# First mixer of a hybrid RG-LRU model: rounding moved to VectorE, splits ahead of square roots, decay series in the prologue, output-projection splits on GpSimd

## The chip, the cores and the metric

The kernel runs on one core of a Trainium2 chip. The metric is the device time of one execution in microseconds (us), as the median of several runs. TensorE (PE) does the matmuls, VectorE (DVE), ScalarE (ACT) and GpSimd (POOL) work on vectors, and SyncE (SP) issues most of the transfers. Each engine takes its own instructions strictly in order; semaphores let one wait for another.

## The reference, cut to what matters

The model has two layers. Layer 0 mixes tokens with a bidirectional gated recurrence (RG-LRU), layer 1 with a chunked gating MLP; each is followed by a mixture-of-experts layer (64 experts, 8 per token). There are 256 latent tokens and 256 context tokens, width 1024. The change lies in the mixer of layer 0:

```python
def lru_coeffs(u, r_w, r_b, i_w, i_b, lam, reset_first):
    r = sigmoid(einsum('bthi,hij->bthj', ub, r_w) + r_b)      # per head, 256x256
    ig = sigmoid(einsum('bthi,hij->bthj', ub, i_w) + i_b)
    log_a = LRU_C * r * log_sigmoid(lam)
    a = exp(log_a)
    mult = sqrt(-expm1(2.0 * log_a))
    return a, mult * ig * u

def rglru_mixer(hx, hc, w_in, conv_w, conv_b, r_w, r_b, i_w, i_b, lam, w_out, ctx_out):
    gate_x, ux = split(hx @ w_in, 2)
    ux = dwconv_centred(ux, conv_w, conv_b)                   # 4 taps
    uc = dwconv_centred(hc @ w_in[:, RNN_WIDTH:], conv_w, conv_b)
    yx = 0
    for d in range(2):                                        # both directions
        h_c = linear_scan(*lru_coeffs(flip(uc), ...))
        a_x, b_x = lru_coeffs(flip(ux), ...)
        b_x[:, 0] += a_x[:, 0] * h_c[:, -1]
        yx = yx + flip(linear_scan(a_x, b_x))
    return (gelu(gate_x) * yx) @ w_out
```

The recurrent width is 1280, in 5 heads of 256 channels. The result is scaled by a modulation vector, which is a matmul of the conditioning vector with large weights (`ada_w`), and added to the stream.

## The kernel before, in words

**Precision.** TensorE takes 32-bit numbers rounded to a shorter form (`F32R`). To keep full precision each operand is split in a high part (rounded) and a low part (the rest), and each product is three matmuls (`mm3`, L309): high by high, high by low, low by high. Weights come from memory as tiles of 128x2048 and are split in four pieces of 128x512 by `splitter` (L553): ScalarE casts the high part `wh` (L563), and VectorE or GpSimd subtracts to give the low part `wl` (L564). Which of the two subtracts is what `split_eng` says (L706): GpSimd for A and C of head 0 and for every second piece of O and Q, VectorE for all else. There are 7 buffers for each part. `wq(q)` emits splits up to piece q + 2, so `ready(n)` emits all pieces below n. Since every engine keeps its order, the place where a split is emitted sets its place in the queues of ScalarE and of the subtracting engine.

**Stages.** A prologue computes the normalisation and, in four quarters of 256 channels, the modulation (`first_quarter`, L718): ada matmuls, VectorE's normalise (L694), ScalarE's high part of the normalised input (L733), VectorE's low part (L744), and A's matmuls of head 0 on the quarters that are there. Then `plan0` lists the steps: for each head h

- A(h): input projection of the recurrent branch, two banks of 128x512 (latent and context tokens beside each other), then the convolution: ScalarE's first tap (L758), VectorE's three others (L760), the rounding `us` (L763, ScalarE) and its low part (L764, VectorE). At its end `roots` (L847) takes the square roots of the results that the head before has left (ScalarE, with a load of another function table).
- C(h): the gate projection, GELU on ScalarE, and `release` (L887): B_end of the head before, the scans on VectorE.
- B(h): the two gates of the recurrence (`T`, `I`), on the weights of the tile "gate", with tanh and exp on ScalarE, then four passes of 128x1024 on VectorE (L841 to L844). `gated` (L894) multiplies with GELU's result and splits into `zh` and `zl`, on GpSimd for heads 0 to 3, on VectorE for head 4.

Between these stand fillers F, the ada matmuls of later modulations (`s<-wr,stat` and `b<-wr,stat`), one tile of weights each. In the order of TensorE: A0 F C0 B0 F, A1 FFF C1 FF B1 F, A2 FF C2 FF B2 F, A3 FF C3 FF B3 F, A4 F C4 FF B4 FFFF. Then O0 to O3 do the output projection for the first four heads, Q adds head 4, and `Tail` (L575) adds to the stream, squares, and starts the router's matmuls.

**Decay.** `decay` (L790) computes log-sigmoid of `lam`, 128x20 numbers, as a series of small GpSimd steps, with one reciprocal (L795) and the last two steps on VectorE (L805, L806). It is called after A0 and before C0's and B0's work.

**Order of transfers.** Weight tiles go through 8 slots in the order of the plan, issued by SyncE; a tile's transfer starts when the tile eight before it has been freed.

Of the kernel before, what the change touches and what calls it, by code (L numbers as in the profile page):

```python
# [301 lines left out]
def _body(nc, tc, a, pp, rp, ps, ps1, dr):  # L302
# [334 lines left out]
    def mixer0(rx):  # L637
      with tc.tile_pool(name="m0", bufs=1) as mp, tc.tile_pool(name="m0t", bufs=2) as tp:
# [26 lines left out]
        for t_, n_ in ((cw, "a_cw"), (cb, "a_cb"), (rb_, "a_rb"), (ib_, "a_ib"), (lam, "a_lam")):  # L665
            nc.sync.dma_start(t_, a[n_])

# [38 lines left out]
        def split_eng(i, c):  # L706
            kind, j = plan0[users[i]]
            return G if kind in "AC" and j == 0 or kind in "OQ" and c % 2 else V

# [4 lines left out]
        def ready(n):  # L714

            wq(n - 3)

        def first_quarter(b):  # L718
# [30 lines left out]
        def A(h, q):  # L749
# [4 lines left out]
            def conv(i, p):  # L754
# [7 lines left out]
                of = o.rearrange("p s t -> p (s t)")  # L762
                S.copy(out=us[:, 0, i, :], in_=of)  # L763
                V.tensor_tensor(out=us[:, 1, i, :], in0=of, in1=us[:, 0, i, :].bitcast(F32), op=OP.subtract)  # L764
# [3 lines left out]
            for i, k in steps:  # L768
                if h == 0 and i == 0 and k:
                    yield  # L770
                wc = divmod(2 * k + i if h == 0 else 8 * i + k, 4)
                mm3(ps_[i], *cut(wq(q + wc[0], 4 if h == 0 and k < 7 else None), wc[1]), h0(0, k), h0(1, k), k == 0, k == 7)
                if k == 7:
                    ready(q + 8)
                    conv(i, ps_[i])
            roots()

# [4 lines left out]
        for b in range(1, 4):  # L782
            for _ in range(NEXT[b - 1]):
                next(a0)
            normalise(range(2 * b, 2 * b + 2))
            first_quarter(b)
        for t_ in (rb_, ib_):
            V.tensor_scalar(out=t_, in0=t_, scalar1=0.5, scalar2=None, op0=OP.mult)

        def decay():  # L790

            S.activation(out=s0, in_=lam, func=AF.Abs)
            S.activation(out=s0, in_=s0, func=AF.Exp, scale=-1.0)
            G.tensor_scalar(out=s1, in0=s0, scalar1=2.0, scalar2=None, op0=OP.add)
            V.reciprocal(out=s1, in_=s1)  # L795
            G.tensor_tensor(out=s0, in0=s0, in1=s1, op=OP.mult)
            G.tensor_tensor(out=s1, in0=s0, in1=s0, op=OP.mult)
            nterm = 9
            G.memset(s2, 1.0 / (2 * nterm + 1))
            for i in range(nterm - 1, -1, -1):  # L800
                G.tensor_tensor(out=s2, in0=s2, in1=s1, op=OP.mult)
                G.tensor_scalar(out=s2, in0=s2, scalar1=1.0 / (2 * i + 1), scalar2=None, op0=OP.add)
            G.tensor_tensor(out=s2, in0=s2, in1=s0, op=OP.mult)
            G.tensor_scalar(out=s1, in0=lam, scalar1=0.0, scalar2=-2.0, op0=OP.min, op1=OP.mult)
            V.scalar_tensor_tensor(out=nz, in0=s2, scalar=4.0, in1=s1, op0=OP.mult, op1=OP.add)  # L805
            V.tensor_scalar(out=nz2, in0=nz, scalar1=-2.0, scalar2=None, op0=OP.mult)  # L806

        def B(h, q):
# [92 lines left out]
        def O(i, q):  # L901
            ob[i] = bank()
            for j in range(2):
                for f in range(8):
                    mm3(ob[i][:, j * T:(j + 1) * T], *cut(wq(q + 2 * j + f // 4), f % 4), zh[:, f, :], zl[:, f, :],
                        j == 0 and f == 0, False)
            if i < 2:
                ready(q + 7)
                release()

# [12 lines left out]
        for i, (kind, j) in enumerate(plan0):  # L923
            if kind == "F":
# [3 lines left out]
                continue  # L928
            if kind == "O" and j == 0:
                tail = Tail(tp, 0, mod[:, 0, 2, :], rw, "hf", 4)  # L930
# [5 lines left out]
            if i == 0:  # L936
                deque(a0, 0)
                decay()
                continue
# [710 lines left out]
```

## Time and profile before

| what | us |
|---|---|
| median of 3 runs | 1522.29 (1521.48 to 1526.03) |
| profiled execution, its own time | 1523.33 |
| its span on the core | 1521.5 |
| PE busy | 1409.8 (93%) |
| DVE busy | 750.9 (49%) |
| ACT busy | 522.9 (34%) |
| POOL busy | 330.2 (22%) |
| prologue, to the end of A0 | 0 to 43.5 |
| heads 0 to 4, to the end of B4 | 43.5 to 224.5 |
| last fillers, O and Q | 224.5 to 277.3 |
| all that follows | 277.3 to 1521.5 |

The span is the time from the first to the last instruction in the trace; the execution's own time also has what lies around it. Busy shares are means over the span; the first mixer, some 277 us, has gaps of PE of its own, which the page's mean hides. In a timeline row the bracket at the end gives the idle time of the engine just before and the engine, tile and line that ended it.

### The profile page before, as it was taken

The page shows a single profiled execution, that of the slowest core. Times are in us where ns is not written, and L with a number is a line of the kernel's source. Part 1 is how long each engine was busy: PE and PEld are TensorE (multiplying, and loading weights), DVE is VectorE, ACT ScalarE, POOL GpSimd, SP SyncE. Part 2 cuts the span into 40 slices and gives each one's busy share as a digit, 9 for nine tenths or more (in the row PEclk, how much of TensorE's full clock was granted, in tenths as well). Part 3 has the DMA queues.
Part 4 walks back from the last instruction along what each step waited for, and adds up shares of the span by engine and source line. Part 5 has one row for each costly group of instructions (what it writes and reads, how often), then busy time and mean ns, then how long its engine had stood idle before and what let it go on. Part 6 is the DMA issues. An engine that isn't in the chain of part 4 may idle for free.

```text
span 1521.5 us, 27414 instructions
## 1 busy us (share of the span) xinstructions
PE 1409.8 (93%) x10752; PEld 983.7 (65%) x10752; DVE 750.9 (49%) x1412; ACT 522.9 (34%) x911; POOL 330.2 (22%) x420
## 2 busy tenths in 40 slices
PE   6798987789999999999999999978999999999998
PEld 4576757646557666565656899855656657566665
DVE  6488888622434433243345697542425334343434
ACT  4676764412322222222224535332213212222232
POOL 1200013421312222112201181232132212121210
PEclk9899998899999999999999999999999999999999
DMA  9575566559998999999999954449999999999994
GB/s 377 240 269 221 222 255 280 232 227 369 353 412 363 421 420 382 421 394 421 421 418 398 346 194 140 165 172 386 372 369 389 386 420 421 403 405 421 420 421 187
DMA packets 77444, 514.86 MB, mean 338 GB/s; under 512 B 9856, under 2 KB 10240, under 8 KB 17024
## 3 DMA queue, kind: packets, MB, share of 16 engines
q1 hardware_dynamic: 74720, 508.91, 82.8%
q10 hardware_dynamic: 2592, 4.16, 0.9%
q8 instruction: 86, 1.41, 0.4%
q14 instruction: 46, 0.38, 0.1%
HBM read 511.99 MB, written 1.05 MB: 337 GB/s over the span
## 4 chain that ended last, share of the span: by engine, by line
PE 56%; issue 13%; DMA 4%; POOL 3%; DVE 2%; ACT 1%; ACTq 0%; POOLq 0%; SPq 0%; DVEq 0%
PE b L307 46%; PE s L307 9%; DMA wr<-in_m_gu 3%; POOL S L1427 2%; POOL wl L564 1%; DMA wr<-in_m_dn 1%; PE b L1503 1%; DMA wx<-in_m_dn 1%; DVE wl L564 1%; DVE h L976 0%; ACT wh L563 0%; DVE v L1032 0%; DVE xT L1143 0%; DVE v L1095 0%; DVE u L984 0%
## 5 line engine op out<-in xcount | busy, mean ns | idle before, releaser
L307 PE MATMUL b<-wr,xg 128*32 128x512 f32 (+2 forms) x1512 | 306.8, 599 | 9.2 <-DMA wr<-in_m_gu 8.0
L564 POOL TENSOR_TENSOR wl<-wr,wh 128x512 fp32r<-128x512 f32 x81 | 111.5, 1388 | 560.2 <-ACT wh L563 533.3
L563 ACT CAST wh<-wr 128x512 fp32r<-128x512 f32 x260 | 152.1, 618 | 164.1 <-PE s L307 79.8
L564 DVE TENSOR_TENSOR wl<-wr,wh 128x512 fp32r<-128x512 f32 x179 | 141.1, 815 | 125.9 <-ACT wh L563 125.8
L307 PE MATMUL b<-wx,xg 128*32 128x512 f32 (+2 forms) x696 | 199.2, 598 | 0.9 <-ACT xg L1443 0.7
L307 PEld LDWEIGHTS b<-wr,xg 128*32 128x32 f32 (+2 forms) x1512 | 84.5, 118 | 141.3 <-issue 114.2
L307 PE MATMUL s<-hh,wh 128*128 128x256 f32 x512 | 153.1, 299 | 6.4 <-ACT wh L563 6.4
L307 PE MATMUL b<-wr,ht 128*32 128x512 f32 (+2 forms) x728 | 153.8, 596 | 2.7 <-ACT ht L1505 1.4
L1143 DVE SCALAR_TENSOR_TENSOR xT<-b,mod,xT 128x256 f32<-128x256 f32 x304 | 130.0, 479 | 48.9 <-PE b L307 43.0
L1519 DVE SCALAR_TENSOR_TENSOR Y<-b,gt,Y 128x512 fp32r<-128x512 f32 x88 | 66.1, 751 | 169.3 <-ACT Y L1518 169.3
L307 PE MATMUL s<-hh,wl 128*128 128x256 f32 x512 | 146.3, 286 | 3.4 <-POOL wl L564 3.4
L307 PE MATMUL s<-hl,wh 128*128 128x256 f32 x512 | 145.3, 284 | 0.0
L564 POOL TENSOR_TENSOR wl<-wx,wh 128x512 fp32r<-128x512 f32 x43 | 58.5, 1367 | 299.3 <-ACT wh L563 258.7
L307 PEld LDWEIGHTS s<-hh,wh 128*128 128x128 f32 x512 | 98.8, 193 | 36.0 <-issue 28.3
L1496 DVE TENSOR_TENSOR h<-h,b 128x256 f32<-128x256 f32 x44 | 18.5, 421 | 208.2 <-ACT h L1495 208.2
L1518 ACT ACTIVATE Y<-b,gt 128x512 fp32r<-128x512 f32 x88 | 60.5, 687 | 136.6 <-PE b L307 132.2
L1495 ACT ACTIVATE h<-b 128x256 f32<-128x256 f32 x44 | 16.9, 383 | 259.8 <-PE b L307 259.8
L307 PE MATMUL b<-wx,ht 128*32 128x512 f32 (+2 forms) x376 | 101.9, 596 | 0.8 <-ACT ht L1505 0.5
L307 PEld LDWEIGHTS s<-hh,wl 128*128 128x128 f32 x512 | 98.7, 193 | 4.5 <-POOL wl L564 4.2
L563 ACT CAST wh<-wx 128x512 fp32r<-128x512 f32 x108 | 64.6, 619 | 101.9 <-PE s L307 51.7
L307 PEld LDWEIGHTS s<-hl,wh 128*128 128x128 f32 x512 | 99.0, 193 | 0.4
L307 PE MATMUL b<-S,xt 128*128 128x256 f32 x704 | 94.1, 287 | 0.0
(283 smaller groups left out, 2773.9 us busy)
## 6 DMA issues: line engine op xcount, KB each, us to landing
wr<-in_m_gu SPq DMA_DIRECT2D x170, 1024.0 KB, 11.9
wx<-in_m_gu SPq DMA_DIRECT2D x86, 1024.0 KB, 12.1
wr<-in_m_dn SPq DMA_DIRECT2D x82, 1024.0 KB, 10.6
wx<-in_m_dn SPq DMA_DIRECT2D x40, 1024.0 KB, 11.3
wr<-in_ada_w SPq DMA_DIRECT2D x32, 1024.0 KB, 7.8
wr<-in_a_in SPq DMA_DIRECT2D x10, 1024.0 KB, 8.3
wr<-in_ada SPq DMA_DIRECT2D x8, 1024.0 KB, 12.2
wr<-in_b_v SPq DMA_DIRECT2D x6, 1024.0 KB, 14.8
```

What stands on the lines that cost most here:

```text
L307: PE.matmul(out, lhsT, rhs, start=start, stop=stop, skip_group_check=True)
L563: S.copy(out=hi, in_=t)
L564: eng(i, c).tensor_tensor(out=lo, in0=t, in1=hi.bitcast(F32), op=OP.subtract)
L1143: V.scalar_tensor_tensor(out=xT[:, d, :], in0=y, scalar=mod[:, l, 5, d:d + 1], in1=xT[:, d, :], op0=OP.mult, op1=OP.add)
L1427: (G if b else V).tensor_scalar(out=s[:, tt, i * P + o:i * P + o + wd], in0=C["iota1"][:, j:j + wd], scalar1=agq[:, tt, q:q + 1], scalar2= ...
L1495: S.activation(out=h, in_=p[:, :256], func=AF.Silu)
L1496: V.tensor_tensor(out=h, in0=h, in1=p[:, 256:], op=OP.mult)
L1503: PE.transpose(p[:, k * P:(k + 1) * P], h[:, k * P:(k + 1) * P], ident)
L1518: S.activation(out=hi, in_=p, func=AF.Copy, scale=gts[g])
L1519: V.scalar_tensor_tensor(out=y[:, 1, 512 * c:512 * c + 512], in0=p, scalar=gts[g], in1=hi.bitcast(F32), op0=OP.mult, op1=OP.subtract)
```

## The change

It touches the first mixer alone:

- The rounding `us` goes from ScalarE to VectorE.
- A emits three of the four splits of the gate tile ahead of `roots` (`ready(q + 11)`), where all four stood behind it.
- `decay` moves into the prologue, behind the second quarter, after three splits for A0 (`wq(1, 4)`). Its last two steps and the halving of the biases `rb_` and `ib_` move from VectorE to GpSimd; the reciprocal stays on VectorE.
- The five small loads (`cw`, `cb`, `rb_`, `ib_`, `lam`) are issued by ScalarE in place of SyncE.
- `split_eng` gives every low part of O to GpSimd and every low part of Q to VectorE.
- O emits its splits ahead of its matmuls, for all four groups, and the releases too.
- `Tail` is made at O2 in place of O0, so the scaling of the router's weights (`rws`) and its first matmuls come later.

```diff
@@ -663,7 +663,7 @@
         nc.sync.dma_start(mixg, a["mix_g"])
         st.grow(rp, "wr", RING)
         for t_, n_ in ((cw, "a_cw"), (cb, "a_cb"), (rb_, "a_rb"), (ib_, "a_ib"), (lam, "a_lam")):
-            nc.sync.dma_start(t_, a[n_])
+            S.dma_start(t_, a[n_])
 
         for half, e in ((0, pe[:, :16].rearrange("p (k r) -> p k r", k=4).unsqueeze(3).to_broadcast([P, 4, 4, 64])),
                         (1, pe[:, 16:].rearrange("p (k c) -> p k c", k=4).unsqueeze(2).to_broadcast([P, 4, 4, 64]))):
@@ -705,7 +705,7 @@
 
         def split_eng(i, c):
             kind, j = plan0[users[i]]
-            return G if kind in "AC" and j == 0 or kind in "OQ" and c % 2 else V
+            return G if kind in "AC" and j == 0 or kind == "O" else V
 
 
         base = 8
@@ -714,6 +714,25 @@
         def ready(n):
 
             wq(n - 3)
+
+        def decay():
+
+            S.activation(out=s0, in_=lam, func=AF.Abs)
+            S.activation(out=s0, in_=s0, func=AF.Exp, scale=-1.0)
+            G.tensor_scalar(out=s1, in0=s0, scalar1=2.0, scalar2=None, op0=OP.add)
+            V.reciprocal(out=s1, in_=s1)
+            G.tensor_tensor(out=s0, in0=s0, in1=s1, op=OP.mult)
+            G.tensor_tensor(out=s1, in0=s0, in1=s0, op=OP.mult)
+            nterm = 9
+            G.memset(s2, 1.0 / (2 * nterm + 1))
+            for i in range(nterm - 1, -1, -1):
+                G.tensor_tensor(out=s2, in0=s2, in1=s1, op=OP.mult)
+                G.tensor_scalar(out=s2, in0=s2, scalar1=1.0 / (2 * i + 1), scalar2=None, op0=OP.add)
+            G.tensor_tensor(out=s2, in0=s2, in1=s0, op=OP.mult)
+            G.tensor_scalar(out=s1, in0=lam, scalar1=0.0, scalar2=-2.0, op0=OP.min, op1=OP.mult)
+            G.tensor_scalar(out=s2, in0=s2, scalar1=4.0, scalar2=None, op0=OP.mult)
+            G.tensor_tensor(out=nz, in0=s2, in1=s1, op=OP.add)
+            G.tensor_scalar(out=nz2, in0=nz, scalar1=-2.0, scalar2=None, op0=OP.mult)
 
         def first_quarter(b):
 
@@ -760,7 +779,7 @@
                     V.scalar_tensor_tensor(out=o[:, :, d0:d1], in0=pv[:, :, s0_:s1_], scalar=cw[:, kk, ft:ft + 1],
                                            in1=o[:, :, d0:d1], op0=OP.mult, op1=OP.add)
                 of = o.rearrange("p s t -> p (s t)")
-                S.copy(out=us[:, 0, i, :], in_=of)
+                V.tensor_copy(out=us[:, 0, i, :], in_=of)
                 V.tensor_tensor(out=us[:, 1, i, :], in0=of, in1=us[:, 0, i, :].bitcast(F32), op=OP.subtract)
 
             ps_ = [bank(), bank()]
@@ -773,6 +792,7 @@
                 if k == 7:
                     ready(q + 8)
                     conv(i, ps_[i])
+            ready(q + 11)
             roots()
 
         held, rooted, done = deque(), deque(), []
@@ -784,27 +804,11 @@
                 next(a0)
             normalise(range(2 * b, 2 * b + 2))
             first_quarter(b)
+            if b == 1:
+                wq(1, 4)
+                decay()
         for t_ in (rb_, ib_):
-            V.tensor_scalar(out=t_, in0=t_, scalar1=0.5, scalar2=None, op0=OP.mult)
-
-        def decay():
...
-            V.scalar_tensor_tensor(out=nz, in0=s2, scalar=4.0, in1=s1, op0=OP.mult, op1=OP.add)
-            V.tensor_scalar(out=nz2, in0=nz, scalar1=-2.0, scalar2=None, op0=OP.mult)
-
+            G.tensor_scalar(out=t_, in0=t_, scalar1=0.5, scalar2=None, op0=OP.mult)
         def B(h, q):
             warm(AF.Exp)
             uc, us = ucs.pop(h)
@@ -900,13 +904,13 @@
 
         def O(i, q):
             ob[i] = bank()
+            ready(q + 7)
+            if i < 2:
+                release()
             for j in range(2):
                 for f in range(8):
                     mm3(ob[i][:, j * T:(j + 1) * T], *cut(wq(q + 2 * j + f // 4), f % 4), zh[:, f, :], zl[:, f, :],
                         j == 0 and f == 0, False)
-            if i < 2:
-                ready(q + 7)
-                release()
 
         def Q(_, q):
             wq(q + 1)
@@ -926,7 +930,7 @@
                 ada_step(l, c, k, tp)
                 wq(4 * sum(u < i for u in users) + 1)
                 continue
-            if kind == "O" and j == 0:
+            if kind == "O" and j == 2:
                 tail = Tail(tp, 0, mod[:, 0, 2, :], rw, "hf", 4)
             if kind == "O" and j == 2:
                 warm(AF.Sqrt)
@@ -935,7 +939,6 @@
                     gated(done.pop())
             if i == 0:
                 deque(a0, 0)
-                decay()
                 continue
             n = st.reserve({"A": "a_in", "C": "a_in", "B": "gate", "O": "a_out", "Q": "a_out"}[kind])
             deque({"A": A, "B": B, "C": Cg, "O": O, "Q": Q}[kind](j, 4 * users.index(n - base)) or (), 0)
```

How the rows of the engines move, at three places. ScalarE in head 1, from the convolution to C1's GELU (`uc` convolution, `us` its rounding, `wr_736` and `wr_737` the gate tile of head 1, `Tt` the held results of head 0), before:

```order
L758 ACTIVATE uc<-b,cb,cw 128x512
L763 CAST us<-uc 128x512
L758 ACTIVATE uc<-b,cb,cw 128x512
L763 CAST us<-uc 128x512
L851 ACT_TABLE_LOAD
L851 ACTIVATE Tt<-Tt 128x1024 x2
L563 CAST wh<-wr_736 128x512 x4
L880 ACT_TABLE_LOAD
```

and after:

```order
L777 ACTIVATE uc<-b,cb,cw 128x512 x2
L563 CAST wh<-wr_737 128x512 x3
L855 ACT_TABLE_LOAD
L855 ACTIVATE Tt<-Tt 128x1024 x2
L563 CAST wh<-wr_737 128x512
L884 ACT_TABLE_LOAD
```

Three of the four casts now stand ahead of the table load and the roots, and the two casts of `us` are gone from this queue.

VectorE in the prologue, from the second to the third quarter (`hf` and `wx` the low part of the input, `s_184` the decay's intermediate, `Tt` and `I` normalise), after:

```order
L759 TENSOR_SCALAR hf<-Tt,sx,mod 128x256
L759 TENSOR_SCALAR hf<-I,sc,modc 128x256
L763 TENSOR_TENSOR wx_103<-hf,wx_101 128x512
L723 RECIPROCAL s_184<-s_184 128x20
L694 TENSOR_TENSOR Tt<-xT,b 128x256 x2
```

and GpSimd at the same place, after:

```order
L564 TENSOR_TENSOR wl<-wr_128,wh 128x512 x4
L722 TENSOR_SCALAR s_184<-s_183 128x20
L724 TENSOR_TENSOR s_183<-s_183,s_184 128x20
L725 TENSOR_TENSOR s_184<-s_183 128x20
L727 MEMSET s_185 128x20
```

The reciprocal, which came after A0's convolution before, now stands between two quarters, and it needs GpSimd's first step (`s_184` at L722), which stands behind all four subtracts of A0's tile `wr_128`.

GpSimd from the end of the heads to Q (`zh` and `zl` of heads 2 and 3, `wr_1794` and `wr_1807` the first tile of O), before:

```order
L899 TENSOR_TENSOR zl<-hf,zh 128x512
L564 TENSOR_TENSOR wl<-wr_1794,wh 128x512
L898 CAST zh<-hf 128x512
L899 TENSOR_TENSOR zl<-hf,zh 128x512
L564 TENSOR_TENSOR wl<-wr_1794,wh 128x512
L564 TENSOR_TENSOR wl<-wr_1861,wh 128x512 x2
L564 TENSOR_TENSOR wl<-wx_1889,wh 128x512 x2
L564 TENSOR_TENSOR wl<-wx_1891,wh 128x512 x2
L564 TENSOR_TENSOR wl<-wx_1893,wh 128x512 x2
L618 TENSOR_TENSOR hf<-hf 128x256 x5
```

and after:

```order
L903 TENSOR_TENSOR zl<-hf,zh 128x512
L564 TENSOR_TENSOR wl<-wr_1807,wh 128x512 x2
L902 CAST zh<-hf 128x512
L903 TENSOR_TENSOR zl<-hf,zh 128x512
L564 TENSOR_TENSOR wl<-wr_1807,wh 128x512 x2
L564 TENSOR_TENSOR wl<-wr_1862,wh 128x512 x4
L564 TENSOR_TENSOR wl<-wx_1890,wh 128x512 x4
L564 TENSOR_TENSOR wl<-wx_1892,wh 128x512 x4
L618 TENSOR_TENSOR hf<-hf 128x256 x5
```

Every subtract of O is on this queue now, two of them ahead of head 3's `zh` where one was, and those of Q (the last row of `wx_1893` before) have left it.

## Rows read from the trace of the kernel before

**Rows 1.** Stretches: start to end, length, busy of each engine (count), PEclk, DMA share, GB/s.

```profile
43.50:73.80 30.30, 20.42 (x109) 16.29 (x112) 11.83 (x19) 17.52 (x29) 9.13 (x27) 0.83 0.56 226
...
310.70:1521.50 1210.80, 1155.90 (x9065) 785.88 (x9065) 514.52 (x988) 341.91 (x624) 263.71 (x335) 0.98 0.89 359
```

**Rows 2.** Waits of PE from 43 to 282 us: total, times, longest.

```profile
PE b L307 <- DVE wl L564: 18.8, 5, 7.6
PE b L307 <- ACT wh L563: 13.6, 4, 4.7
```

**Rows 3.** Timeline of PE: start, length, line, operation, tiles, count [idle before, releaser].

```profile
52.68 0.73 PE L307 MATMUL b<-us,wh 128*128 128x512 f32 x2 [2.27 <-ACT wh L563]
61.02 0.79 PE L307 MATMUL b<-us,wl 128*128 128x512 f32 x1 [7.61 <-DVE wl L564]
...
96.58 0.73 PE L307 MATMUL b<-us,wh 128*128 128x512 f32 x2
...
107.69 0.64 PE L307 MATMUL s<-wr,stat 128*32 128x512 f32 x4
...
134.60 1.22 PE L307 MATMUL b<-us,wh 128*128 128x512 f32 x2 [4.73 <-ACT wh L563]
...
148.53 1.06 PE L307 MATMUL s<-wr,stat 128*32 128x512 f32 x7
...
172.40 0.73 PE L307 MATMUL b<-us,wh 128*128 128x512 f32 x2 [1.83 <-ACT wh L563]
...
211.27 1.22 PE L307 MATMUL b<-us,wh 128*128 128x512 f32 x2 [4.73 <-ACT wh L563]
...
224.47 1.06 PE L307 MATMUL s<-wr,stat 128*32 128x512 f32 x8
...
242.22 0.58 PE L307 MATMUL b<-zh,wl 128*128 128x256 f32 x1 [6.21 <-DVE wl L564]
...
259.69 0.39 PE L307 MATMUL b<-zh,wl 128*128 128x256 f32 x1 [3.98 <-DVE wl L564]
...
266.76 0.28 PE L307 MATMUL b<-zh,wh 128*128 128x256 f32 x1
...
277.32 1.07 PE L307 MATMUL b<-wr,stat 128*32 128x512 f32 x8
```

**Rows 4.** A stretch behind the wait of B2, columns as in rows 1.

```profile
135.00:139.00 4.00, 4.00 (x10) 3.02 (x10) 3.92 (x8) 3.97 (x7) 0.00 (x0) 0.50 0.24 35
```

**Rows 5.** Timeline of DVE, end of head 2's convolution.

```profile
130.76 0.69 DVE L764 TENSOR_TENSOR us<-uc,us 128x512 fp32r<-128x512 f32 x1 [0.74 <-ACT us L763]
134.58 2.50 DVE L564 TENSOR_TENSOR wl<-wr,wh 128x512 fp32r<-128x512 f32 x4 [3.13 <-ACT wh L563]
```

**Rows 6.** Timeline of DVE, output projection.

```profile
224.73 0.69 DVE L897 TENSOR_TENSOR hf<-hf 128x512 f32<-128x512 f32 x1
...
232.54 2.31 DVE L841 SCALAR_TENSOR_TENSOR Tt<-T,Tt 128x1024 f32<-128x1024 f32 x1
...
235.61 1.22 DVE L843 SCALAR_TENSOR_TENSOR Tt<-Tt 128x1024 f32<-128x1024 f32 x1
...
257.88 0.43 DVE L898 CAST zh<-hf 128x512 fp32r<-128x512 f32 x1
```

**Rows 7.** Timeline of DVE, third quarter of the prologue and end of decay.

```profile
30.86 0.75 DVE L694 TENSOR_TENSOR Tt<-xT,b 128x256 f32<-128x256 f32 x2
...
59.99 0.18 DVE L805 SCALAR_TENSOR_TENSOR nz<-s,s 128x20 f32<-128x20 f32 x1 [7.19 <-POOL s L804]
```

**Rows 8.** Timeline of POOL, prologue.

```profile
30.34 2.98 POOL L564 TENSOR_TENSOR wl<-wr,wh 128x512 fp32r<-128x512 f32 x2 [5.91 <-ACT wh L563]
```

**Rows 9.** Timeline of ACT's queue, a transfer that it issues.

```profile
1.16 0.46 ACTq L417 DMA_DIRECT2D ccs<-in_cc  x1
```

**Rows 10.** Timeline of POOL, output projection.

```profile
232.18 1.58 POOL L564 TENSOR_TENSOR wl<-wr,wh 128x512 fp32r<-128x512 f32 x1 [1.78 <-ACT wh L563]
```

**Rows 11.** Groups by line, POOL, 200 to 280 us: count, busy, mean ns, idle before, releasers.

```profile
L564 POOL TENSOR_TENSOR wl<-wx,wh 128x512 fp32r<-128x512 f32 x8 | 11.0, 1380 | 19.0 <-ACT wh L563 19.0
```

More of the change, by code (lines that the diff above doesn't have):

```diff
@@ L786, in mixer0 @@
             first_quarter(b)
+            if b == 1:
+                wq(1, 4)
+                decay()
         for t_ in (rb_, ib_):
-            V.tensor_scalar(out=t_, in0=t_, scalar1=0.5, scalar2=None, op0=OP.mult)
-        def decay():
[L792 to L804, printed above, removed]
-            V.scalar_tensor_tensor(out=nz, in0=s2, scalar=4.0, in1=s1, op0=OP.mult, op1=OP.add)
-            V.tensor_scalar(out=nz2, in0=nz, scalar1=-2.0, scalar2=None, op0=OP.mult)
+            G.tensor_scalar(out=t_, in0=t_, scalar1=0.5, scalar2=None, op0=OP.mult)
         def B(h, q):
```

## The prediction

> **What bounds the kernel now.** I read the table by stretches first. From 310.7 us to the end TensorE is busy 1155.90 of 1210.8 us [rows 1]; nothing of the change lies there, and the diff leaves TensorE's order in that part as it was, so I take the rest as shifted and read only the first mixer. The list of waits of TensorE in that stage is short: 18.8 us in five waits for VectorE's low parts (`wl`, L564) and 13.6 us in four for ScalarE's high parts (`wh`, L563) [rows 2]. These 32 us are what the change can win. The timeline places them: 2.27 and 7.61 at the gates of head 0 (B0), 4.73 at B2 (134.60), 1.83 at B3 (172.40), 4.73 at B4 (211.27), 6.21 in the second output-projection group O1 (242.22), 3.98 in O3 (259.69) [rows 3]. What is left of the 18.8 after 7.61, 6.21 and 3.98 is 1.0 in two short waits ahead of B4. B1 (96.58) has no wait and takes 107.69 - 96.58 = 11.1 us [rows 3]: my measure for a gate group.
>
> A wait costs more than itself. B2 goes from 134.60 to 148.53, 13.9 us, 2.8 over B1; B4 from 211.27 to 224.47, 13.2, 2.1 over [rows 3]. Behind the wait of B2 the granted clock is 0.50, the 1.2 GHz level [rows 4]. B0, from 52.68 to the end of its stretch at 73.8 [rows 1, 3], takes 21.1; less the 7.61 inside and 11.1, 2.4 is clock.
>
> **The change, part by part.**
>
> *Splits ahead of the roots, rounding on VectorE.* In VectorE's row ahead of B2 the last convolution low part is computed at 130.76 after 0.74 us of waiting for ScalarE's cast; then VectorE stands 3.13 us, until ScalarE has done the square roots, before it subtracts the four gate pieces (2.50) [rows 5]. The new order casts three pieces ahead of the roots, and the rounding costs VectorE one cast, 0.43 [rows 6], instead of the 0.74 of waiting: 0.3 won per tile, twice per head. Had the cast no better price than a two-input instruction, 0.69, it would still cost no more than the wait; as upper bound I keep 1.22, a pass over twice the size [rows 6]. VectorE stood in head 1 too, while TensorE didn't wait there; so at B2 it is ahead by that 3.13 and about 1.0 of casts besides what TensorE gained. Its convolution ends at 131.45 (130.76 + 0.69) [rows 5], and B2's low part is wanted 0.4 after 129.87 (134.60 - 4.73) [rows 3]: 1.2 late today, 4.1 ahead recovered, less the first subtract's 0.62, so 2.3 spare. I take the whole 4.73 and the 2.8 of clock: **B2 7.5**. B3's 1.83 goes alike: **1.8**. At B4 1.0 + 4.73 + 2.1 = 7.8, less 0.7 that I keep for VectorE as the late one (between nothing and the 2.50 of its four subtracts), less two hits of 1.1 (below), for the first pieces of O0 are split on GpSimd there: **4.9**.
>
> *Decay early.* Today VectorE stands 7.19 behind the GpSimd series (59.99) and the gate subtracts queue behind it [rows 7]: that is the 7.61. Without it B0 wins 2.27 + 7.61 + 2.4 = 12.3. The price is in the prologue. VectorE's reciprocal now stands in its queue ahead of the third quarter's normalise, which starts at 30.86 today without a wait [rows 7]. The reciprocal needs GpSimd's first step, which stands behind three subtracts. Two of these take 2.98 from 30.34 [rows 8]; the third makes 34.8, and ScalarE's share of the delay 1.3 makes 36.1, so normalise starts near 36.4 in place of 30.86: 5.5 late. From there VectorE works to the end of the prologue nearly without idle time, so TensorE's head 0 is late by as much. The 1.3: five small loads are issued by ScalarE ahead of the first squares, at 0.46 each [rows 9], 2.3 in all, of which I take 1.0 as lying in a wait it had for data; bounds 0 and 2.3. The synchronising engine is relieved of five issues; its weight loads wait for a round of older transfers, so no gain. With 0.6 for one subtract (a quarter of 2.50 [rows 5]) that now falls just behind the convolution, **head 0: 12.3 - 5.5 - 0.6 = 6.2**. If the reciprocal waits for nothing, it is 11.7.
>
> Behind the reciprocal GpSimd runs the series, 7.2 us [rows 7], and then four subtracts for C0. C0 ends where B0's first wait begins, at 50.4 today (52.68 - 2.27) [rows 3] and 55.9 then, and wants its last low part some 1.4 before that. It is ready at 36.4 + 7.2 + about 0.5 for the halving of the biases, two small steps, + four times 1.49 [rows 8] = 50.1: 4 us of slack. I cost the series at nothing; that slack is the cover, and what it doesn't cover C0 and B0 are late by.
>
> *Output projection.* So far 6.2 + 7.5 + 1.8 + 4.9 = **20.4** by the end of B4. VectorE's product of head 3 moves from 224.73 to 204.3 [rows 6]. From there it works without a break to the low part of head 4, which Q needs: the cast at 257.88, 0.43, and 0.69 like the product: 259.0, so 34.3 today [rows 6]. The change takes five subtracts out (0.62 each, a quarter of 2.50 [rows 5], 3.1) and the router-weight product (0.69 like its kind). It adds interference: GpSimd now does 14 of the pieces in this stretch for 8. The pair to read: GpSimd's subtract at 232.18 takes 1.58 [rows 10] and VectorE's pass at 232.54 2.31, where one like it took 1.22 at 235.61 [rows 6]: 1.09 more, about what was left of GpSimd's instruction. Six more such are 6.5, bounds 0 and 8.3 (six at 1.38 [rows 11]). So 34.3 - 3.8 + 6.5 = 37.0, the low part of head 4 is ready at 241.3, and Q's third matmul, behind the router-weight product and one subtract (0.69 each), at 242.7. Waits inside O (6.21, 3.98) vanish, for VectorE no longer makes those parts, but TensorE then waits once, at Q, until 242.7, with low clock behind it. Q runs today from 266.76 to 277.32, 10.6 [rows 3]; with 1.8 of low clock, which I take below B4's 2.1, it ends at 254.9 (0.2 of it ahead of the third matmul). **277.3 - 254.9 = 22.4.**
>
> A rule bears on the 1.09: the Trainium skill ("SBUF — State Buffer", on the two sides of SBUF) says that VectorE with two inputs in SBUF and GpSimd take their common port pair as a lock, and the loser is fully blocked for the whole instruction. The pair of rows agrees: 1.22 from 232.54 to GpSimd's end at 233.76, then 1.22 of work, would give 2.44, and 2.31 is shown. It speaks against this part of the change, and it is the mechanism of the first two rivals.
>
> **Sum.** The profiled run took 1523.33 (span 1521.5); less 22.4, 1500.9. The median of the runs is 1.0 lower: **1500**.
>
> **Rivals.**
> 1. *The series is stretched by the same port.* The 27 small GpSimd steps run beside VectorE's third and fourth quarter. If every one waits out an instruction of 0.69, that is 18.6, less 4 of slack 14.6: 1515. If every second, 9.3 - 4 = 5.3: 1505. For: VectorE hardly pauses there. Against: the pair at 232 shows one GpSimd instruction that started first and was not held up by much (1.58 against a mean of 1.38) [rows 10, 11], and many of VectorE's steps there have one input from SBUF. I put its time between the two, at 1509.
> 2. *Every piece blocks VectorE whole.* 14 at 1.38 less today's 8 at 1.09 is 10.6 for 6.5: 4.1 later, 1504.
> 3. *VectorE wasn't the last:* the gate pieces wait for their tile's landing, or the roots for the held results, and the 13 us of `wh` waits come back under another name. Then 6.2 and O's part are left, 1513. Against: the 3.13 ends with the cast that follows the roots, not with a transfer [rows 5].
> 4. *Slower: GpSimd paces the output projection.* From 205.0 it has the two parts of head 3, which I count as two pieces (2.8), and then 14 pieces in a row. Q is reached before 242.7 while a piece takes under (242.7 - 207.8)/14 = 2.5; at 4.0 they end at 264, Q 12.4 later, and all the gain is gone; at 5 Q ends at 290, 13 after today: 1536. For: nothing else splits O now. Against: the mean of eight is 1.38 [rows 11], and 2.5 would need each to be blocked for its own length again.
>
> **How the numbers follow.** About 0.3% (4.6 us) is what a measurement can tell from no change. Forecast 0.62, rival 1 0.12, rival 2 0.10, rival 3 0.06, rival 4 0.04, and 0.06 for two or three of rivals 1 to 3 together, which leave near no change. Faster is the forecast with rivals 1 to 3, 0.90; same 0.06; slower 0.04. Range: with no prologue wait (5.5) and half of the hits (3.3) 1491; towards the slow side rivals 1 to 3 to 1512. So 1490 to 1512.
>
> **What would show it.** Right: no wait of TensorE at B2, B3 and B4 over 1 us, none of 7 us in B0; VectorE's reciprocal with an idle time of about 5 us ahead of it near 36 us and C0 late by 5 to 6; granted clock 1.00 behind the gates; one wait of 6 to 10 us at Q, ended by VectorE. Wrong: a reciprocal that waits for nothing, GpSimd steps far over 0.3 us each in the series, a wait in O ended by GpSimd's `wl`, or a wait at B2 ended by a transfer.

## The result

The changed kernel takes 1501.07 us (median of 4 runs, 1497.05 to 1508.41); the kernel before, beside it, 1521.88 (1519.88 to 1526.03). The ratio is 0.9865, 95% interval 0.9822 to 0.9909: faster by 1.4%. The forecast was 1500.0, in a range of 1490 to 1512. So the time came out; the experiments below show that two of the forecast's accounts did not: what held up B2 to B4, and what the early decay is worth beside the other parts.

The page of the changed kernel (span; busy time, share and instructions of each engine): VectorE's busy time has hardly changed, GpSimd's has grown by 17 us, and the span is 21.7 shorter.

```profile
span 1499.8 us, 27427 instructions
...
PE 1406.8 (94%) x10752; PEld 983.8 (66%) x10752; DVE 754.1 (50%) x1412; ACT 517.5 (35%) x901; POOL 347.2 (23%) x431
```

Its stretches (columns as in [rows 1]): the prologue, head 2, the end of the mixer, all that follows. The last has a length of 1244.4; before it was 1521.5 - 277.32 = 1244.2 [rows 1, 3]. All of the difference lies ahead of it. Head 2 (from B1's end to B2's end) has no idle time of PE now, at clock 1.00. The prologue has become longer (43.5 before).

```profile
0.00:49.80 49.80, 30.78 (x329) 23.63 (x330) 29.09 (x80) 22.14 (x38) 17.12 (x40) 0.90 0.94 366
...
101.80:134.90 33.10, 33.10 (x186) 24.60 (x185) 32.17 (x49) 25.03 (x38) 1.54 (x1) 1.00 0.68 258
...
202.70:255.40 52.70, 44.24 (x333) 39.31 (x332) 43.49 (x48) 23.73 (x40) 31.42 (x21) 0.94 0.65 252
255.40:1499.80 1244.40, 1180.67 (x9253) 807.83 (x9252) 539.41 (x1080) 359.33 (x658) 283.24 (x361) 0.98 0.88 356
```

The waits of PE from 40 us to Q's end (total, times, longest) answer to [rows 2]. Where 18.8 and 13.6 us stood, there are 2.2 and 1.2; new are the wait for head 4's high part at Q and five short ones for GpSimd's low parts in O. The two for `wx` lie in the prologue.

```profile
PE b L307 <- DVE zh L902: 3.0, 1, 3.0
PE b L307 <- POOL wl L564: 2.7, 5, 0.8
PE b L307 <- ACT wx L752: 2.6, 2, 1.6
PE b L307 <- DVE wl L564: 2.2, 3, 1.0
PE b L307 <- ACT wh L563: 1.2, 1, 1.2
```

PE's timeline at the marks of [rows 3]: end of A0 (43.47 before), B0, B2, B4, Q's begin, Q's end.

```profile
49.79 1.16 PE L307 MATMUL s<-wr,stat 128*32 128x512 f32 x8
67.89 1.07 PE L307 MATMUL s<-wr,stat 128*32 128x512 f32 x8
...
134.90 1.06 PE L307 MATMUL s<-wr,stat 128*32 128x512 f32 x8
...
202.68 2.78 PE L307 MATMUL s<-wr,stat 128*32 128x512 f32 x24
...
239.89 0.36 PE L307 MATMUL b<-zh,wh 128*128 128x256 f32 x1 [2.99 <-DVE zh L902]
...
255.41 6.21 PE L307 MATMUL b<-wr,stat 128*32 128x512 f32 x56
```

### The profile page after: what moved, and what is told of

The parts are those of the page before. It is cut to its first block, busy times and chain, and to the rows that moved or that the text cites. A ratio compares the mean times of both kernels' runs of the same rounds, so it can differ in the third digit from the quotient of the medians.

```text
span 1499.8 us, 27427 instructions
## 1 busy us (share of the span) xinstructions
PE 1406.8 (94%) x10752; PEld 983.8 (66%) x10752; DVE 754.1 (50%) x1412; ACT 517.5 (35%) x901; POOL 347.2 (23%) x431
## 3 DMA queue, kind: packets, MB, share of 16 engines
q8 instruction: 86, 1.41, 0.4%
## 4 chain that ended last, share of the span: by engine, by line
PE 57%; issue 15%; POOL 3%; DMA 3%; DVE 2%; ACT 1%; ACTq 0%; POOLq 0%; SPq 0%; DVEq 0%
PE b L307 46%; PE s L307 9%; POOL S L1430 2%; POOL wl L564 1%; DMA wr<-in_m_gu 1%; DMA wr<-in_m_dn 1%; DMA wx<-in_m_dn 1%; PE b L1506 1%; DVE wl L564 1%; DVE h L979 0%; ACT wh L563 0%; PE b L1618 0%; DVE v L1035 0%; DVE xT L1146 0%; DVE v L1098 0%
## 5 line engine op out<-in xcount | busy, mean ns | idle before, releaser
L564 POOL TENSOR_TENSOR wl<-wr,wh 128x512 fp32r<-128x512 f32 x85 | 119.6, 1420 | 545.7 <-ACT wh L563 542.2
L564 POOL TENSOR_TENSOR wl<-wx,wh 128x512 fp32r<-128x512 f32 x45 | 63.7, 1430 | 281.4 <-ACT wh L563 242.4
L1430 POOL TENSOR_SCALAR S<-cst,agq 128x32 fp32r<-128x32 f32 (+3 forms) x208 | 83.6, 427 | 49.7 <-PE b L307 49.7
```

The lines of the kernel that those rows point to most:

```text
L564: eng(i, c).tensor_tensor(out=lo, in0=t, in1=hi.bitcast(F32), op=OP.subtract)
L1430: (G if b else V).tensor_scalar(out=s[:, tt, i * P + o:i * P + o + wd], in0=C["iota1"][:, j:j + wd], scalar1=agq[:, tt, q:q + 1], scalar2= ...
```

## The experiments

Executions of one kernel spread by 3 to 12 us, and in the profiled ones what follows Q takes 1237.7 to 1247.4, so small differences are read from the marks in the trace. One trace is kept of each kernel, and the prologue varies from one to the next: the kernel in the row "... and O shared" ends A0 at 45.2, the three other kernels with the same prologue at 42.5 to 42.8. All in us; "Q" is the time from B4's end to Q's end.

| kernel | A0 ends | B0 ends | B4 ends | Q ends | Q | median | ratio (95%) |
|---|---|---|---|---|---|---|---|
| before | 43.5 | 73.8 | 224.5 | 277.3 | 52.8 | 1521.9 | 1 |
| changed | 49.8 | 67.9 | 202.7 | 255.4 | 52.7 | 1501.1 | 0.987 (0.982 to 0.991) |
| roots first | 48.5 | 67.9 | 202.7 | 255.7 | 53.0 | 1501.6 | 0.987 (0.982 to 0.992) |
| decay as before | 44.4 | 65.1 | 201.0 | 253.4 | 52.4 | 1498.0 | 0.983 (0.979 to 0.987) |
| decay first | 47.3 | 66.5 | 201.2 | 253.1 | 51.9 | 1498.8 | 0.985 (0.981 to 0.989) |
| loads on SyncE | 46.4 | 65.8 | 200.6 | 253.8 | 53.2 | 1496.9 | 0.984 (0.981 to 0.988) |
| rounding and splits undone | 49.8 | 68.2 | 219.9 | 272.4 | 52.5 | 1518.3 | 0.998 (0.996 to 1.000) |
| rounding undone | 48.9 | 67.9 | 218.6 | 270.9 | 52.3 | 1514.3 | 0.995 (0.992 to 0.998) |
| splits and decay undone | 45.2 | 73.9 | 209.2 | 261.1 | 52.0 | 1506.2 | 0.991 (0.988 to 0.995) |
| decay and loads as before | 42.5 | 63.2 | 198.7 | 250.7 | 52.0 | 1494.8 | 0.982 (0.980 to 0.985) |
| ... and O as before | 42.8 | 63.4 | 198.2 | 251.2 | 52.9 | 1499.6 | 0.985 (0.981 to 0.988) |
| ... and O shared | 45.2 | 65.9 | 200.7 | 254.5 | 53.8 | 1500.6 | 0.984 (0.982 to 0.986) |
| ... and O on VectorE | 42.8 | 63.5 | 198.3 | 248.4 | 50.1 | 1495.7 | 0.982 (0.979 to 0.984) |
| rounding alone | 43.5 | 72.8 | 206.5 | 262.1 | 55.6 | 1506.5 | 0.990 (0.986 to 0.993) |

The ratio is always to runs of the kernel before on the same chip.

**Roots first.**

```diff
-            ready(q + 11)
             roots()
```

> The changed kernel, but with all four splits of the gate tile behind the square roots again. Theory (the roots ahead of the splits made TensorE wait at B2, B3 and B4): waits for ScalarE's wh of 3 to 5 us come back at B2 and B4 and a smaller one at B3, with granted clock 0.50 behind the larger ones; B4 ends 11 to 15 us later and the kernel takes 1512 to 1517 us. Rival (it was the rounding on VectorE, which stays here, that freed the gate groups): waits under 1 us and 1501 to 1504 us.

The rival was right: B4 ends at 202.72, and no wait for `wh` comes back at B2 to B4. ScalarE's timeline at head 2 shows why. The changed kernel:

```profile
114.33 0.78 ACT L777 ACTIVATE uc<-b,cb,cw 128x512 f32<-128x512 f32 x1 [4.82 <-PE b L307]
115.00 1.65 ACT L563 CAST wh<-wr 128x512 fp32r<-128x512 f32 x3
```

and this run:

```profile
114.35 0.78 ACT L777 ACTIVATE uc<-b,cb,cw 128x512 f32<-128x512 f32 x1 [4.82 <-PE b L307]
115.14 1.28 ACT L854 ACT_TABLE_LOAD   x1
116.44 2.01 ACT L854 ACTIVATE Tt<-Tt 128x1024 f32<-128x1024 f32 x2
118.35 2.16 ACT L563 CAST wh<-wr 128x512 fp32r<-128x512 f32 x4
```

The roots cost their 3.3 us in both. But they start right behind the second convolution tap, so the casts are done at 120.5, and VectorE comes to these pieces only at 121.15, behind its convolution, with no wait. In the kernel before the table load started at 130.74, behind a cast that had waited for VectorE:

```profile
130.11 0.62 ACT L763 CAST us<-uc 128x512 fp32r<-128x512 f32 x1 [2.44 <-DVE uc L760]
130.74 1.28 ACT L851 ACT_TABLE_LOAD   x1
```

**Rounding and splits undone; rounding undone.** The theory was changed to: either of the two suffices.

```diff
-                V.tensor_copy(out=us[:, 0, i, :], in_=of)
+                S.copy(out=us[:, 0, i, :], in_=of)
```

(in the first run together with the edit above).

> The changed kernel with both the early splits and the rounding on VectorE undone: four splits behind the square roots, the rounding us on ScalarE. Theory, changed after the first runs (either of the two alone frees the gate groups, since with the rounding off ScalarE its roots start some 3.7 us earlier; only undone together do they bring the wait back): waits for wh of 3 to 5 us at B2 and B4, low clock behind them, B4 ends 11 to 15 us later than the 202.7 of the changed kernel, 1511 to 1517 us. Rival (it is the early decay that put VectorE ahead, and neither of the two matters): waits under 1.5 us, 1500 to 1504 us.

> The changed kernel with the rounding us on ScalarE again, the early splits kept. Theory (either alone suffices): three casts of the gate pieces follow the second us cast at once, VectorE loses 0.3 us per tile, so B4 ends within 2 us of 202.7 and the time is 1500 to 1504 us. Rival (the rounding on VectorE is the part that matters, since ScalarE's cast waits for VectorE's convolution and what stands behind it is late): waits of 2 to 5 us at B2 and B4, 1508 to 1516 us.

Undone together they bring the waits back as expected, here at B2:

```profile
130.46 1.22 PE L307 MATMUL b<-us,wh 128*128 128x512 f32 x2 [4.73 <-ACT wh L563]
```

They cost 17.2 us at B4's end, more than the 11 to 15 expected. But the rounding undone alone costs 15.9, so "either alone suffices" fell too: the rounding does it, and with the rounding on ScalarE the early splits save 1.3. What ScalarE waits for (the first line of the view from 60 us on, to 220 us for the kernel before and to 200 us for the run with the rounding undone and for the changed kernel, in that order) says it:

```profile
ACT us L763 <- DVE uc L760: 42.1, 8, 9.2
```

```profile
ACT us L782 <- DVE uc L779: 40.0, 7, 9.2
```

```profile
ACT uc L777 <- PE b L307: 18.1, 4, 4.8
```

The cast of `us` was the instruction of ScalarE that waited longest in a head, up to 9.2 us, for VectorE's convolution, and all behind it waited too: the second tap, the roots, the gate casts, and with them VectorE again. Each engine held the other up once per head. With early splits alone three gate casts get ahead of the roots, but still behind this cast (PE waits 1.4 to 1.7 us for `wh` at B2 to B4), the fourth behind the roots, and VectorE's scans behind that, and PE waits another 1.7 to 2.0 us in each of these gate groups for ScalarE's tanh:

```profile
137.32 0.73 PE L307 MATMUL b<-us,wh 128*128 128x512 f32 x2 [1.81 <-ACT T L837]
```

**Rounding alone.** One line of the change, on the kernel before.

> The kernel before with one line of the change, the rounding us on VectorE. Theory (the rounding alone frees the gate groups of heads 2 to 4, the wait for the decay in B0 stays): no wait for ScalarE's wh over 1 us at B2, B3 and B4; B0 keeps a wait for VectorE's wl of 7.5 to 9 us; B4 ends 16 to 19 us before the 224.5 of the kernel before; output projection as before, 52 to 54 us; time 1503 to 1508 us. Rival (without the early splits the roots still hold up the gates when nothing else of the change is there): waits for wh of 2 us and more at B2 and B4, 1511 us or more.

As the theory had it up to B4: heads 2 to 4 have no wait for `wh`, the wait in B0 stays (8.94), and B4 ends 18.0 us earlier than before. The time is 1506.5. With the early splits added and nothing else (the row "... and O as before"), that wait goes too, and B4 ends another 8.3 earlier, at 198.2: these two parts win 26.2 at Q's end, more than the whole change. With the rounding alone O takes 55.6, longer than the 54 expected: the wait in O1 is 7.9 in place of 6.2; the rest of this difference was not followed.

```profile
59.86 0.80 PE L307 MATMUL b<-us,wl 128*128 128x512 f32 x1 [8.94 <-DVE wl L564]
```

**Decay as before.**

```diff
-            if b == 1:
-                wq(1, 4)
-                decay()
...
                 deque(a0, 0)
+                decay()
```

with the last two steps and the bias halving on VectorE.

> The changed kernel with the decay series after A0 again, its last two steps and the halving of the biases on VectorE as before. Theory (moving it won about 12 us at B0 and lost about 5 in the prologue, where VectorE's reciprocal waited): A0 ends at 44 to 46 us, the wait of 7 us for VectorE's wl in B0 is back with low clock behind it, and the kernel is 5 to 8 us slower, 1506 to 1509. Rival A (the move gives back in the prologue all that it wins): 1500 to 1502. Rival B (no price in the prologue): 1512 to 1514.

Against the theory and both rivals, this is no slower than the changed kernel; in the trace B4 ends 1.7 us earlier. The prologue's price is gone (A0 ends at 44.4), and the wait of 7.6 us does not return, though VectorE still stands 7.21 behind the series. Three gate subtracts are queued ahead of the reciprocal now; only the fourth is behind the series, and PE reaches that one just 1.13 us early. VectorE's rows:

```profile
52.26 1.89 DVE L564 TENSOR_TENSOR wl<-wr,wh 128x512 fp32r<-128x512 f32 x3
54.07 0.27 DVE L723 RECIPROCAL s<-s 128x20 f32<-128x20 f32 x1
61.54 0.18 DVE L733 SCALAR_TENSOR_TENSOR nz<-s,s 128x20 f32<-128x20 f32 x1 [7.21 <-POOL s L732]
```

**Splits and decay undone.** The edit of the roots-first run on top of the last one.

> The changed kernel with both the early splits and the early decay undone; the rounding stays on VectorE. Theory (the wait of 7.6 us in B0 can go either by the early decay or by gate splits that are queued on VectorE ahead of the decay's last steps; the run with the decay as before kept three of them ahead and showed 1.1 us): VectorE's gate subtracts stand behind the decay's last step again, B0 has a wait for wl of 4 to 7.5 us with low clock behind it, B4 ends 4 to 8 us after the 201.0 of the run with the decay as before, 1502 to 1507 us. Rival (the wait in B0 had gone for another reason, the rounding on VectorE): waits under 2 us in B0, 1497 to 1500 us.

The theory holds, with more than it expected: without either, the wait is back, larger (8.98, for 4 to 7.5), and B4 ends 8.2 us after that of "decay as before" (for 4 to 8). So the early splits and the early decay each remove this wait, and the change has both.

```profile
61.63 0.79 PE L307 MATMUL b<-us,wl 128*128 128x512 f32 x1 [8.98 <-DVE wl L564]
```

**Decay first.** ScalarE's steps, GpSimd's first and the reciprocal go behind the first quarter's normalise, the series behind the first GpSimd subtract.

```diff
                     normalise(range(2))
+                    decay()
...
                     wq(-2)
+                    series()
```

> The changed kernel with the decay split in two: its ScalarE steps, GpSimd's first step and VectorE's reciprocal right after the first quarter's normalise, the series right after GpSimd's first subtract. Theory (the price in the prologue is the reciprocal that waits behind three subtracts): the idle time of 3.9 us ahead of the reciprocal is gone, A0 ends 4 us earlier (45 to 46 in place of 49.8), and the kernel takes 1496 to 1498 us. Rival (the prologue is late because of the five loads on ScalarE and of the weights that come later): A0's end and the time stay within 1 us. Second rival (small GpSimd steps beside VectorE's quarters cost as much as the wait did): series far over 9 us, no gain.

The reciprocal waits for nothing, as the theory said, but A0's end moves by 2.5 us, not by 4. Of the 2.5, 1.3 is low clock in the changed kernel's trace (next run): against roots first, which has the changed kernel's prologue without it, it is 1.2. The series pushes A0's three subtracts to 34.1, where they meet VectorE's third quarter; its smallest steps (0.16 and 0.41 otherwise) take over 1.2 us each beside them:

```profile
34.14 1.26 DVE L494 TENSOR_TENSOR mod<-hf,adab 128x4 f32<-128x4 f32 x1
...
36.68 1.36 DVE L764 TENSOR_SCALAR hf<-Tt,sx,mod 128x256 f32<-128x256 f32 x1
```

**Loads on SyncE.**

```diff
-            S.dma_start(t_, a[n_])
+            nc.sync.dma_start(t_, a[n_])
```

> The changed kernel with the five small loads issued by SyncE again. Theory (ScalarE's issues hold up its first squares by about 1 us and let the second quarter's weights come later): squares 1 us earlier, A0 ends 1.0 to 1.5 us earlier, 1499.5 to 1500.5 us, which is less than the runs tell apart, so it is read from the trace. Rival (the loads were in the way of SyncE's weight loads): A0 ends later, waits of TensorE for in_ada grow, 1502 to 1505.

Right in direction, too small in size: A0 ends 3.4 us earlier. VectorE's reciprocal comes at 34.20 in place of 36.32, so 2.1 are the loads' price there. The other 1.3 is clock: from 45.8 to 49.6 us, just before the end of A0, the changed kernel shows a granted clock of 0.61, roots first, with the same prologue, 1.00 up to its A0's end at 48.5. These 1.3 are gone by the end of B0, 67.9 in both; the 2.1 stay (65.8 here), and between the two kernels with the decay as before they are 1.9 (65.1 and 63.2). The 2.1 is more than ScalarE's issues account for, which put its squares 1.1 later (7.95 for 6.87 before). In the changed kernel SyncE's queue stands as well: its load of `cst` is issued at 6.72, here at 3.06, and the first weights of the prologue at 10.35, here at 5.83:

```profile
6.72 0.33 SPq L661 DMA_DIRECT2D cst<-in_cst  x1
...
10.35 0.91 SPq L325 DMA_DIRECT2D wr<-in_ada  x2
```

TensorE waits 2.23 and 1.68 for the second quarter's weights there (0.64 and 1.41 here), and from 23 to 29.5 us its granted clock is 0.50 there and 1.00 here. Why SyncE's queue stands was not followed. In the time this run's median gains 4, within what the intervals allow for none.

**Decay and loads as before.** Both edits.

> The changed kernel with the decay as before and the five small loads on SyncE, so that of the change the rounding, the early splits and the output projection's part are left. Theory (both undone parts cost in the prologue and win nothing that the early splits don't): A0 ends at 43.4 to 44.0 us, B0's end is 0.5 to 1.0 us before that of the run with the decay as before (65.1), B4 ends at 199.8 to 200.6, Q at 252 to 253, and the kernel is 2 to 3 us faster than the changed one in the trace. Rival (loads on SyncE let the decay's inputs come late, so that ScalarE waits for lam): A0 or B0 later than 65.1.

A0 ends even earlier than expected (42.5), B4 at 198.7, Q at 250.7: 4.7 us before the changed kernel. The decay alone accounts for 2.6 at B0's end and 1.9 at B4's (65.8 and 200.6 with the loads on SyncE alone). Of the change this kernel keeps the rounding, the early splits and the part in O.

**O as before, shared, on VectorE.** Three runs on this last kernel; in all the decay and the loads are as before.

```diff
-            return G if kind in "AC" and j == 0 or kind == "O" else V
+            return G if kind in "AC" and j == 0 or kind == "O" and c % 2 else V
```

is the shared one; on VectorE, no piece of O is on GpSimd; in the first also emission, Q and tail are as they were.

> The kernel before with only the rounding on VectorE and the early splits; it is the last run's kernel with the output projection's part undone (splits of O and Q shared by GpSimd and VectorE, emitted behind O's matmuls, tail at O0). It measures what that part is worth. Theory from the forecast (it wins 2.0 us from B4's end to Q's end): the stretch from B4's end to the router's first matmuls after Q takes 54 us, against 52.0 in the last run and 52.9 before, and the kernel 1496 to 1498 us. Rival (a wash, since what VectorE is spared it loses to the common port): 51.5 to 52.9 us, 1494 to 1496 us.

> The last run's kernel (decay and loads as before) with every second piece of O split on VectorE in place of GpSimd; emission ahead of the matmuls, Q on VectorE and the late tail stay. Theory (a piece on GpSimd costs VectorE 0.98 us of blocking, a piece on VectorE 0.62 of work): VectorE's chain from head 3's product to head 4's low part, 36.4 us in the last run, falls by 3 to 4, but the last pieces of O3 then follow it on VectorE and TensorE has 4 us of O3 behind it, so Q's end stays within 1.5 us of 250.7. Rival (blocking costs less than the work): chain 36 or longer and Q's end 1.5 us or more later.

> The last run's kernel with all pieces of O split on VectorE, none on GpSimd. Theory (blocking 0.98 against work 0.62 a piece): no VectorE pass in the stretch is over its usual length by more than 0.2 us except beside GpSimd's parts of head 3, the chain from head 3's product to head 4's low part takes 30 to 32 us, and Q's end is 248 to 252, since O3 and a piece of O2 then stand behind that chain. Rival (GpSimd is needed, VectorE alone paces O): waits of TensorE for VectorE's wl of over 5 us in O and Q's end 254 or later.

From B4's end to Q's end they take 52.9, 53.8 and 50.1 us, against 52.0 with all on GpSimd. In this stretch the change's part in O is worth 0.9, at the edge of the rival's range, not the theory's 2.0. But two pieces of O0 come ahead of B4's end, and with both on GpSimd two of VectorE's scans there are held up (1.61 for 0.75 in this one; with O as before one is):

```profile
191.98 1.61 DVE L864 TENSOR_TENSOR_SCAN hf<-T,Tt,I 128x256 f32<-128x256 f32 x1
```

B4 ends 0.8 later for it. From B3's end, which these edits leave alone, to Q's end it takes 87.5 us with all on GpSimd, and 87.7, 88.5 and 84.8 in the three runs: the change's part in O is a wash, as the rival had it, and the opposite choice is 2.7 to 2.9 shorter than either. Putting O's splits ahead of its matmuls and making the tail late were not undone by themselves. In the shared run TensorE waits 7.75 for a low part of VectorE in O1, and 2.7 of its late Q's end (254.5, for 252.2 expected at most) lie ahead of A0's end, by chance. VectorE's chain from head 3's product to head 4's low part takes 34.2, 32.7 and 28.0, against 36.4: it falls further than expected on VectorE alone. Three passes of 128x1024 in the changed kernel, two beside GpSimd's subtracts and one without:

```profile
210.33 2.30 DVE L848 SCALAR_TENSOR_TENSOR I<-I,uc 128x1024 f32<-128x1024 f32 x1
212.56 2.30 DVE L845 SCALAR_TENSOR_TENSOR Tt<-T,Tt 128x1024 f32<-128x1024 f32 x1
...
218.70 1.21 DVE L848 SCALAR_TENSOR_TENSOR I<-I,uc 128x1024 f32<-128x1024 f32 x1
```

and GpSimd's subtracts at that time, where one takes 2.02 us, and later 1.71, where [rows 11] had 1.38:

```profile
207.59 10.10 POOL L564 TENSOR_TENSOR wl<-wr,wh 128x512 fp32r<-128x512 f32 x5
```

```profile
221.68 13.71 POOL L564 TENSOR_TENSOR wl<-wx,wh 128x512 fp32r<-128x512 f32 x8
```

With none on GpSimd the same two passes are at 1.22:

```profile
205.56 1.22 DVE L844 SCALAR_TENSOR_TENSOR I<-I,uc 128x1024 f32<-128x1024 f32 x1
206.70 0.68 DVE L564 TENSOR_TENSOR wl<-wr,wh 128x512 fp32r<-128x512 f32 x1
207.30 1.22 DVE L841 SCALAR_TENSOR_TENSOR Tt<-T,Tt 128x1024 f32<-128x1024 f32 x1
```

A piece on GpSimd takes 1.0 to 1.1 from VectorE (2.30 against 1.21) and a piece on VectorE 0.6. This kernel, with decay and loads as before and O on VectorE, is the earliest at Q's end: 248.4, 7.0 us before the changed one. Its time, 1495.7, and the 1494.8 of the kernel with O on GpSimd are not to be told apart.

## Why the prediction was right, and where its reasons were not

- **Sum.** Forecast gain 22.4 at Q's end, measured 277.32 - 255.41 = 21.9. What follows kept its length, as assumed.
- **B2 7.5, B3 1.8, B4 4.9.** Measured 7.8 (40.8 to 33.1 from B1's end to B2's end), 2.2 and 6.0. The sizes were near, the cause was not right. The step that failed is "ScalarE has done the square roots": the 3.13 of [rows 5] does end with the cast behind the roots, but the roots were late because ScalarE's rounding had waited for VectorE. The rounding was booked at "0.3 won per tile"; undoing it alone costs 15.9, and made alone on the kernel before it wins 18.0 at B4's end. The early splits, to which the prediction gave these waits, win nothing at B2 to B4 beside it; what they can win is in B0, the wait that the prediction gave to the decay. The sum was insensitive to this, since the waits go in either account: that is luck. A chain of waits between two engines has to be followed one step further than to the instruction that ends it.
- **Decay, 12.3 - 5.5 - 0.6 = 6.2.** Measured 5.9 at B0's end, with A0 6.3 late: 12.2 won against 6.3. The prologue's mechanism was right, the reciprocal at 36.32 after 3.93 idle (36.1 forecast):

```profile
36.32 0.28 DVE L723 RECIPROCAL s<-s 128x20 f32<-128x20 f32 x1 [3.93 <-POOL s L722]
```

  Mis-sized were the loads, 1.3 for 2.1, with "its weight loads wait for a round of older transfers, so no gain", which missed that ScalarE's loads now stand in SyncE's way; and low clock at A0's end, 1.3, was not counted (nor did it cost anything by B0's end). What failed is the crediting: "Without it B0 wins 2.27 + 7.61 + 2.4 = 12.3" is near what a kernel without the rounding and the early splits shows (18.4 us from A0's end to B0's end, against 30.3 before); beside them the early decay loses 1.7 at B4's end (2.8 at B0's). The prediction never asked what each part is worth once the others are in.
- **Output projection 2.0 (20.4 to 22.4).** Measured 0.1, at 21.8 by B4's end. VectorE's chain was right: 37.0 forecast, 36.45 measured (204.02 to 240.47), and so was the place of Q's wait. That the waits inside O vanish was not: GpSimd paces the pieces, the first five at 2.02 us each, and PE waits 2.7 in five of them, one of the prediction's own signs of being wrong, and 1.2 for ScalarE. In place of one wait of 6 to 10 us at Q there are 2.99 and 1.02. Q's third matmul comes at 241.93 (242.7 forecast), but from there to Q's end it takes 13.5 us, for a forecast of 12.2: the term for low clock, 1.8, was too small, for the clock stays low until 248.

```profile
241.00:248.00 7.00, 5.88 (x26) 5.59 (x27) 4.09 (x10) 0.81 (x2) 0.73 (x1) 0.51 0.41 150
```

  That two errors, the gain by B4's end too small by 1.4 and that of O too large by 1.9, cancel, is luck.
- **Rivals.** The first (the series stretched) shows in part: the series takes 9.7 us from 36.69 to 46.36 with its new last steps, where it took 7.2, and four small steps there take 0.65 to 0.74 in place of 0.25; C0 had the slack. Of the second, every piece does hold up a step of VectorE, but by 1.0 to 1.1, the forecast's price, not by 1.38: the chain takes 36.45, for 37.0 forecast and 41.1 by this rival. The fourth (GpSimd paces O) did not decide: 2.02 a piece in the slowest stretch, for the 2.5 where it would have. The third did not occur.

The Trainium skill's rule ("SBUF — State Buffer", "SBUF: two separate sides") says that when GpSimd and a VectorE instruction with two inputs in SBUF meet, the one that starts first has their common port pair for its whole instruction, and the other is blocked. These rows agree that both sides lose: VectorE's passes grow by 1.1 and GpSimd's subtracts from 1.38 to 2.02.

## What to carry to other kernels

When a wait ends at an engine that did other work first, look at what that engine itself waited for (its own list of waits), before crediting the work: here one cast that crossed from VectorE to ScalarE and back held up both, and moving it to the engine that makes its input was worth more than all reordering. Test the parts of a change one by one and in pairs: two of the four parts removed the same wait, and each of them, undone alone, looked worthless or costly. Work handed to GpSimd to spare VectorE is charged with what it takes from VectorE while both run (1.0 to 1.1 us for a piece of 0.6 here).

## What the runs showed that was not expected

- Moving five small loads to ScalarE's queue made SyncE's own issues stand still for 3.7 us (`cst` at 6.72 for 3.06). All seven kernels with these loads on ScalarE show it (6.5 to 6.9), none of the seven with them on SyncE; why stays open.
- VectorE steps on 4 numbers a partition (1.26 for 0.16), and passes with one tensor input (L846, 1.65 to 1.68 for 0.69), are held up by GpSimd's subtract as long as two-input passes of 128x1024 (2.30 for 1.21): about 1 us each.
- Without any early split the gate groups B2 to B4 run without a wait for ScalarE's high parts, once the rounding is on VectorE.
